# Block 1's mixers: POOL's tensor operations written for DVE, and the norm's factor applied in the copy out of PSUM

## The chip, the cores and the metric

The kernel runs on one core of a Trainium2 chip. The metric is device time in microseconds (us) of the whole program, lower is better. TensorE (PE, and PEld for its weight loads) multiplies matrices into PSUM; VectorE (DVE), ScalarE (ACT) and GpSimd (POOL) work element by element; SyncE (SP) issues the DMA transfers.

## The reference

Two transformer-like blocks on a sequence of 1024 tokens of width 1024, in float32. Only block 1's first half, the mixers, is touched by the change:

```python
h = rms_norm(x, norm_mix[l])
proj = jnp.einsum("bsd,dc->bsc", h, w_in[l])
q, k, v, z, b_f, b_b, a_f, a_b, su, sv = jnp.split(proj, SPLIT_POINTS, axis=-1)
qkv = jax.nn.silu(short_conv(jnp.concatenate([q, k, v], axis=-1), conv_w[l]))
o_a = bidir_gated_deltanet(qkv, z, b_f, b_b, a_f, a_b, ...)   # 8 heads of 64, chunks of 64
o_b = spatial_gating(su, sv, ...)                             # 4 groups of 128
x = x + jnp.einsum("bsc,cd->bsd", jnp.concatenate([o_a, o_b], axis=-1), w_out[l])
```

`rms_norm` multiplies each token by one factor, so the factor can be applied before the product with `w_in` or to the product. The delta rule solves a unit triangular system for each chunk, head and direction, and then runs over 16 chunks in order. After the mixers come block 1's feed-forward network and all of block 2 (an S5 state space layer, a gated convolution and a second feed-forward network).

## The kernel before

Tiles hold 128 channels by 1024 tokens, handled in two halves of 512 (`HS`). Every dense product is made of three float32r products: weight and input are both split into a high part (ACT copies it, line 318) and a low part (a subtraction, line 319), and hi·hi, hi·lo and lo·hi are summed in PSUM. `piece` loads one weight block (`wr`) and splits it (`wh`, `wl`); the engine of the subtraction is an argument. There are two buffers of `wr` and three each of `wh` and `wl`, so ACT's next `wh` waits until PE has used up an older one. Outputs of products go through two PSUM banks (`mm`), and for some of the products through two spare ones.

`norm0` splits the input and sums its squares over the 8 tiles (line 407) while the first products run; its factor per token is spread over the partitions in `rb`. The products are made on the unnormalised input, and the factor is multiplied in afterwards: `evac` copies both halves of a product out of PSUM on ACT (line 753) and POOL multiplies the copy by `rb` (line 754). `conv_tile` then makes one convolved tile of 128 channels: ACT the middle tap, DVE four taps (line 764), ACT a tanh, ACT adds 1 (line 767), POOL multiplies (line 768).

The heads go in four pairs. `pair_front` makes a pair's q, k and v, `pair_gdn` its delta rule: decays (DVE adds at line 901, POOL masks by `affine_select` at 905, ACT exponentials), Gram products, the inverse of the 32 by 32 diagonal blocks (31 steps of two DVE operations, lines 957 and 959, each step on the result of the last), the off-diagonal block, and the chain over the chunks (lines 1074 and 1077). Two pairs run at a time, pairs 0 and 1, then 2 and 3. `sgu_mix` makes the gated groups.

PE's program order is written out while the kernel is built: `drive` interleaves the steps of the two pairs, of the gated groups and of the dense products by constants for their latencies. The order on DVE, ACT and POOL is made by a scheduler from the same program; `late` and `at` bias it. Each engine works through its own order, and waits at an instruction whose inputs aren't there, with all that stands behind it.

Of the kernel before, what the change touches and what calls it, by code (L numbers as in the profile page):

```python
# [16 lines left out]
P = 128  # L17
# [234 lines left out]
class Kern:  # L252
# [69 lines left out]
    def front(self):  # L322
# [16 lines left out]
        with tc.manual_schedule(engines={mybir.EngineType.PE}):  # L339
            self.mark("norm")  # L340
            with self.pool("n0") as n0:
                self.norm0(n0)
            self.gp = es.enter_context(self.pool("gp", reuse_waits="tile"))
            self.gdn_consts()
            self.drive(self.dense(xes, res_es))
            self.tailw = [self.piece(I["w_out"], 2 * P, d * P, 2, G, 2 * P) for d in (0, 2, 4)]
        es.close()
        return self.res, res_es

    def norm0(self, n0):  # L350
# [16 lines left out]
        self.dma(self.ident, self.I["c_ident"])  # L367
        w0[2] = self.piece(wi, HF, 512, 4, G)
        w0[0] = self.piece(wi, 0, 2048, 8, G, 32, raw=n0.tile([P, HF], F32, name="wg"))
        load(0, (4, 6))  # L370
# [21 lines left out]
        for h in range(2):  # L392
# [3 lines left out]
            for d in range(KD):  # L396
# [9 lines left out]
                if d:  # L406
                    G.tensor_tensor(acc, acc, t, op=ALU.add)
                if h == 0:
# [58 lines left out]
    def mix_split(self, m, i, j):  # L467

        t = [self.rp.tile([P, S], F32R, tag=f"mx{i}{j}{e}", name="mix", bufs=1) for e in range(2)]
        for h in range(2):  # L470
            sl = self.HS[h]
            self.split(t[0][:, sl], t[1][:, sl], m[:, sl], (self.G, self.V)[(j + h) % 2])
        return t
# [105 lines left out]
    def wout(self, k0, mix, d, hs=(0, 1)):  # L579

        self.mark("wout")
        pss = yield from self.gprod(self.I["w_out"], k0 * P, d * P, mix, self.G, hs)
        for h, ps in zip(hs, pss):
# [47 lines left out]
    def proj(self, c0):  # L631
        if c0 in self.pre:
            return self.pre.pop(c0)
        return (yield from self.gprod(self.I["w_in"], 0, c0, self.x, self.G))

# [113 lines left out]
    def evac(self, pss, name):  # L749
        t = self.f4(name)  # L750
        with self.at(self.PR_EVAC):
            for h in range(2):
                self.A.activation(t[:, self.HS[h]], pss[h], AF.Copy)
        self.G.tensor_tensor(t, t, self.rb, op=ALU.mult)
        return t

    def conv_tile(self, j, raw, y):
# [8 lines left out]
        A.activation(raw, y, AF.Tanh)  # L766
        A.activation(raw, raw, AF.Copy, bias=1.0)
        self.G.tensor_tensor(y, raw, y, op=ALU.mult)
        return y
# [88 lines left out]
    def pair_gdn(self, p, st, R):  # L858
# [90 lines left out]
        for eg, dst in ((i_, i_), (K, Q)):  # L949
            self.late(A.activation(eg, eg, AF.Exp))  # L950
            G.tensor_tensor(dst, eg, Q, op=ALU.mult)
        for j in range(31, 0, -1):
# [15 lines left out]
        Y = [g, hs]  # L968
        for d, eng in ((0, V), (1, G)):
            eng.tensor_tensor(Y[d].rearrange("p (c e k) -> p c e k", e=2, k=32),  # L970
                              yc[:, d].unsqueeze(2).to_broadcast([P, NC, 2, 32]),
# [28 lines left out]
        for lo_, hi_ in zip(lo, hi):  # L1000
            A.activation(c3(Y[1])[hi_, :, 0:32], yp[hi_], AF.Copy, scale=-1.0)
        G.tensor_tensor(c3(K), c3(kp), bc(3), op=ALU.mult)

# [26 lines left out]
        for d in range(2):  # L1030
            G.tensor_tensor(c3(KW[d]), c3(kp), bc(4 + d), op=ALU.mult)
        one = lambda t, sl: t[:, sl].rearrange("p (c k) -> p c k", k=64)
# [140 lines left out]
    def sgu_mix(self):  # L1173
# [10 lines left out]
        for g in range(4):  # L1184
# [19 lines left out]
            v8 = vq.rearrange("p (n c) -> p n c", n=8)  # L1204
            G.tensor_tensor(v8, v8, r.unsqueeze(2).to_broadcast([P, 8, P]), op=ALU.mult)
            yield 0.0, self.LAT_SGU[1]
            t = vr
            for h in range(2):
                sl = self.HS[h]
                ps = yield from bank([P, 4, P], "mix")  # L1210
                for n in range(4):
# [4 lines left out]
                                       ws[:, 1:2, :].to_broadcast([P, 4, P]), op0=ALU.mult, op1=ALU.add)  # L1216
                G.tensor_tensor(gu[:, sl], gu[:, sl], t[:, sl], op=ALU.mult)
                A.activation(t[:, sl], gu[:, sl], AF.Square)
# [1108 lines left out]
```

## Time and profile before

| | us |
|---|---|
| median of 3 runs | 2793.81 (2791.37 to 2794.6) |
| the profiled execution | 2792.41 |
| its span, first to last instruction | 2790.5 |
| busy in the span: PE, DVE, ACT, POOL | 2616.2, 1861.0, 1076.9, 576.4 |

The mixers take about the first 795 us of the span. A stretch of the span is read by what is busy in it: an engine that is busy all the time sets the pace there, and a gap on PE is put down to the instruction that ended it.

### The profile page before, as it was taken

What the parts mean: (1) busy time and instruction counts of PE and PEld (TensorE: products, weight loads), DVE (VectorE), ACT (ScalarE), POOL (GpSimd) and SP (SyncE); (2) the same over time, 40 slices, a digit from 0 to 9 for tenths busy, and PEclk for the clock granted to TensorE, in tenths of its full rate; (3) what the DMA queues carried; (4) which work ended last, traced back from release to release, by engine and by line L of the source; (5) the groups of instructions that cost most, each with busy time, mean ns of one, the idle gap of its engine ahead of it and who ended that gap; (6) DMA issues with size and microseconds to landing.
All of it is one profiled execution on the core that took longest, in us unless ns stands there. A gap on an engine that the chain in (4) does not pass through costs nothing.

```text
span 2790.5 us, 39625 instructions
## 1 busy us (share of the span) xinstructions
PE 2616.2 (94%) x14952; PEld 2094.8 (75%) x14952; DVE 1861.0 (67%) x3174; ACT 1076.9 (39%) x1779; POOL 576.4 (21%) x671
## 2 busy tenths in 40 slices
PE   7777899889999999999999999989999999999997
PEld 4556677666777888888788888778876888888885
DVE  6889658865577666845547888666497555555446
ACT  4544443533264444422125443363245333352212
POOL 5764334523200000089910000100000000000010
PEclk8888999899999999999999999999999999999998
DMA  3332142213124333645422543554422222243211
GB/s 102 89 91 73 36 126 78 79 44 118 55 83 143 120 114 129 203 139 171 141 78 80 164 155 120 181 176 147 132 72 65 79 91 91 76 148 109 89 47 60
DMA packets 298623, 299.73 MB, mean 107 GB/s; under 512 B 34912, under 2 KB 243936, under 8 KB 298176
## 3 DMA queue, kind: packets, MB, share of 16 engines
q1 hardware_dynamic: 298432, 297.20, 34.2%
q8 instruction: 117, 1.92, 0.3%
q14 instruction: 74, 0.61, 0.1%
HBM read 222.29 MB, written 74.58 MB: 106 GB/s over the span
## 4 chain that ended last, share of the span: by engine, by line
PE 74%; DVE 17%; issue 3%; DMA 2%; ACT 2%; POOL 1%; SPq 1%; ACTq 0%; DVEq 0%; POOLq 0%
PE mm L1327 33%; PE mm L1300 28%; PE mm L611 5%; DVE h L959 2%; DVE stp L957 2%; PE wu L775 2%; DVE cy L764 1%; DVE fbgkq L764 1%; PE ob L775 1%; DVE xl L399 1%; PE mm L193 1%; DVE wl L319 1%; PE cp L775 1%; DVE res L216 1%; PE mm L1432 0%
## 5 line engine op out<-in xcount | busy, mean ns | idle before, releaser
L1327 PE MATMUL mm<-t,wh 128*128 128x512 f32 x1728 | 539.9, 393 | 11.3 <-DVE t L319 4.1
L318 ACT ACTIVATE wh<-wr 128x512 fp32r<-128x512 f32 (+1 forms) x386 | 236.0, 613 | 627.6 <-PE mm L1300 267.2
L1327 PEld LDWEIGHTS mm<-t,wh 128*128 128x128 f32 x1728 | 324.3, 188 | 88.5 <-DVE t L319 7.5
L1327 PE MATMUL mm<-b,wh 128*128 128x512 f32 x1232 | 382.5, 392 | 2.9 <-ACT acc L1368 2.9
L1300 PE MATMUL mm<-fh,wh 128*128 128x512 f32 x880 | 345.7, 393 | 4.8 <-DVE res L1508 4.8
L319 DVE TENSOR_TENSOR wl<-wr,wh 128x512 fp32r<-128x512 f32 (+1 forms) x311 | 219.4, 706 | 192.8 <-ACT wh L318 192.5
L1300 PE MATMUL mm<-fl,wh 128*128 128x512 f32 x880 | 343.2, 390 | 0.0
L1300 PE MATMUL mm<-fh,wl 128*128 128x512 f32 x880 | 343.0, 390 | 0.0
L1327 PE MATMUL mm<-t,wl 128*128 128x512 f32 x864 | 337.2, 390 | 0.0
L1327 PEld LDWEIGHTS mm<-b,wh 128*128 128x128 f32 x1232 | 231.5, 188 | 53.1 <-ACT acc L1368 4.0
L1327 PE MATMUL mm<-b,wl 128*128 128x512 f32 x616 | 240.2, 390 | 0.0
L318 ACT ACTIVATE wh<-ws 128x512 fp32r<-128x512 f32 x216 | 135.3, 630 | 252.8 <-PE mm L1327 232.0
L1300 PEld LDWEIGHTS mm<-fh,wh 128*128 128x128 f32 x880 | 165.5, 188 | 41.5 <-issue 5.2
L319 DVE TENSOR_TENSOR wl<-ws,wh 128x512 fp32r<-128x512 f32 x216 | 148.4, 690 | 71.2 <-ACT wh L318 70.8
L611 PE MATMUL mm<-xh,wh 128*128 128x512 f32 (+1 forms) x400 | 175.3, 438 | 21.7 <-ACT rows L826 7.1
L1300 PEld LDWEIGHTS mm<-fh,wl 128*128 128x128 f32 x880 | 165.6, 188 | 34.8
L1300 PEld LDWEIGHTS mm<-fl,wh 128*128 128x128 f32 x880 | 165.6, 188 | 34.4 <-issue 0.5
L1327 PEld LDWEIGHTS mm<-t,wl 128*128 128x128 f32 x864 | 162.8, 188 | 33.7
L319 POOL TENSOR_TENSOR wx<-wr,wx 128x512 fp32r<-128x512 f32 (+1 forms) x8 | 8.6, 1094 | 846.4 <-ACT wx L318 843.4
L611 PE MATMUL mm<-xl,wh 128*128 128x512 f32 (+1 forms) x400 | 172.8, 432 | 4.3 <-DVE xl L399 4.2
L611 PE MATMUL mm<-xh,wl 128*128 128x512 f32 (+1 forms) x400 | 171.7, 429 | 0.0
L319 POOL TENSOR_TENSOR wl<-wr,wh 128x512 fp32r<-128x512 f32 (+1 forms) x75 | 94.3, 1258 | 280.4 <-ACT wh L318 197.8
(498 smaller groups left out, 4758.1 us busy)
## 6 DMA issues: line engine op xcount, KB each, us to landing
wr<-in_w_ff SPq DMA_DIRECT2D x76, 256.0 KB
wr<-in_w_ff SPq DMA_DIRECT2D x32, 512.0 KB
fl<-ffd SPq DMA_DIRECT2D x32, 512.0 KB
wr<-in_w_in SPq DMA_DIRECT2D x32, 512.0 KB
wr<-in_w_in SPq DMA_DIRECT2D x60, 256.0 KB
wr<-in_w_gate SPq DMA_DIRECT2D x22, 512.0 KB
wr<-in_w_up SPq DMA_DIRECT2D x22, 512.0 KB
fl<-hd SPq DMA_DIRECT2D x22, 512.0 KB
```

The source lines that it names most:

```text
L193: K.T.matmul(st[:, e * n + k:e * n + k + 1], x[:, k * P:(k + 1) * P], K.ones[:, 0:1], start=e + i + k == 0, stop=i == 1, skip_group_check= ...
L216: K.V.tensor_tensor(r, r, self.mb, op=ALU.subtract)
L318: self.A.activation(hi, src, AF.Copy)
L319: return (lo_eng or self.V).tensor_tensor(lo, src, hi.bitcast(F32), op=ALU.subtract)
L399: V.scalar_tensor_tensor(xl[d][:, sl], xs[:, d, sl], g, xh[d][:, sl].bitcast(F32), op0=ALU.mult, op1=ALU.subtract)
L611: self.T.matmul(ps, a[:, t, :], b[:, sl], start=(first and j == 0), stop=(last and j == 2))
L764: V.scalar_tensor_tensor(y[:, a:b], raw[:, a + o:b + o], cw[:, k:k + 1], y[:, a:b], op0=ALU.mult, op1=ALU.add)
L775: self.T.matmul(out(s), lhsT(s), rhs(s), start=start, stop=stop)
L957: V.tensor_tensor(tm, X3[:, :, 0:j, j:j + 1].to_broadcast([P, 2, j, n]), T3[:, :, j:j + 1, m:16].to_broadcast([P, 2, j, n]), op=ALU.mult)
L959: V.tensor_tensor(T3[:, :, 0:j, m:16], T3[:, :, 0:j, m:16], tm, op=ALU.subtract)
L1300: self.T.matmul(ps, a, b[:, sl], start=(start and k + j == 0), stop=(stop and k == n - 1 and j == 2))
L1327: self.T.matmul(ps, a[:, k, :], b, start=(start and k + j == 0), stop=(k == 3 and j == 2), skip_group_check=True)
```

## The change

In the mixers every POOL operation on two tensors is written for DVE: the low parts of the weights and of the mixers' outputs, the sums of squares, and the products of the delta rule and of the gated groups. `evac` reads PSUM on DVE and multiplies by `rb` on the way, so that ACT's copy and POOL's multiplication become one DVE instruction for each half. The end of `conv_tile`, (tanh + 1) times y, becomes one DVE instruction in place of one of ACT and one of POOL. POOL keeps `affine_select`, memory fills, one weight block at the mixers' end and its work in block 2.

```diff
@@ norm0 @@
-        w0[2] = self.piece(wi, HF, 512, 4, G)
-        w0[0] = self.piece(wi, 0, 2048, 8, G, 32, raw=n0.tile([P, HF], F32, name="wg"))
+        w0[2] = self.piece(wi, HF, 512, 4, V)
+        w0[0] = self.piece(wi, 0, 2048, 8, V, 32, raw=n0.tile([P, HF], F32, name="wg"))
...
-                    G.tensor_tensor(acc, acc, t, op=ALU.add)
+                    V.tensor_tensor(acc, acc, t, op=ALU.add)
@@ mix_split @@
-            self.split(t[0][:, sl], t[1][:, sl], m[:, sl], (self.G, self.V)[(j + h) % 2])
+            self.split(t[0][:, sl], t[1][:, sl], m[:, sl], self.V)
@@ wout, and the same in proj @@
-        pss = yield from self.gprod(self.I["w_out"], k0 * P, d * P, mix, self.G, hs)
+        pss = yield from self.gprod(self.I["w_out"], k0 * P, d * P, mix, self.V, hs)
@@ evac @@
-                self.A.activation(t[:, self.HS[h]], pss[h], AF.Copy)
-        self.G.tensor_tensor(t, t, self.rb, op=ALU.mult)
+                self.V.tensor_tensor(t[:, self.HS[h]], pss[h], self.rb[:, self.HS[h]], op=ALU.mult)
@@ conv_tile @@
-        A.activation(raw, raw, AF.Copy, bias=1.0)
-        self.G.tensor_tensor(y, raw, y, op=ALU.mult)
+        V.scalar_tensor_tensor(y, raw, 1.0, y, op0=ALU.add, op1=ALU.mult)
@@ pair_gdn, and the same at 1002 and 1031 @@
-            G.tensor_tensor(dst, eg, Q, op=ALU.mult)
+            V.tensor_tensor(dst, eg, Q, op=ALU.mult)
...
-        for d, eng in ((0, V), (1, G)):
-            eng.tensor_tensor(Y[d].rearrange("p (c e k) -> p c e k", e=2, k=32),
+        for d in range(2):
+            V.tensor_tensor(Y[d].rearrange("p (c e k) -> p c e k", e=2, k=32),
@@ sgu_mix, and the same at 1217 @@
-            G.tensor_tensor(v8, v8, r.unsqueeze(2).to_broadcast([P, 8, P]), op=ALU.mult)
+            V.tensor_tensor(v8, v8, r.unsqueeze(2).to_broadcast([P, 8, P]), op=ALU.mult)
```

The order of instructions on PE is the same in both programs. On DVE, where pair 0's inverse begins (`stp` and `h` are its steps, `cy` a convolved tile of another pair, `wl` the low part of a weight block, `raw<-mm` a product read from PSUM), there stood before:

```order
L832 SCALAR_TENSOR_TENSOR rows<-rows,vecs,grow 32x1024
L957 TENSOR_TENSOR stp<-fbgkq,h 128x62
L959 TENSOR_TENSOR h<-h,stp 128x2x31
L957 TENSOR_TENSOR stp<-fbgkq,h 128x60
L959 TENSOR_TENSOR h<-h,stp 128x2x30
L957 TENSOR_TENSOR stp<-fbgkq,h 128x116
L959 TENSOR_TENSOR h<-h,stp 128x2x29x2
L957 TENSOR_TENSOR stp<-fbgkq,h 128x112
L959 TENSOR_TENSOR h<-h,stp 128x2x28x2
L957 TENSOR_TENSOR stp<-fbgkq,h 128x162
L959 TENSOR_TENSOR h<-h,stp 128x2x27x3
```

and there stands now:

```order
L830 SCALAR_TENSOR_TENSOR rows<-rows,vecs,grow 32x1024
L319 TENSOR_TENSOR wl<-wr,wh 128x512
L955 TENSOR_TENSOR stp<-fbgkq,h 128x62
L753 TENSOR_TENSOR raw<-mm,rb 128x512
L766 SCALAR_TENSOR_TENSOR cy<-raw,cy 128x1024
L753 TENSOR_TENSOR raw<-mm,rb 128x512
L957 TENSOR_TENSOR h<-h,stp 128x2x31
L319 TENSOR_TENSOR wl<-wr,wh 128x512
L848 COPY col<-cps 64x8x6 x4
L955 TENSOR_TENSOR stp<-fbgkq,h 128x60
L763 SCALAR_TENSOR_TENSOR cy<-raw,cwh,cy 128x1022
L957 TENSOR_TENSOR h<-h,stp 128x2x30
```

Between two steps of the inverse there are now reads of products, low parts and a convolution's last step, each of them an instruction that waits for ACT or PE. On POOL, from pair 0's masks to pair 1's, there stood before:

```order
L905 AFFINE_SELECT ca<-ca 64x1024 x2
L905 AFFINE_SELECT fbgkq<-fbgkq 64x1024 x2
L905 AFFINE_SELECT ca<-ca 64x1024 x2
L905 AFFINE_SELECT de<-de 64x1024 x2
L319 TENSOR_TENSOR wl<-wr,wh 128x512 x2
L754 TENSOR_TENSOR raw<-raw,rb 128x1024
L768 TENSOR_TENSOR fbgkq<-raw,fbgkq 128x1024
L319 TENSOR_TENSOR wl<-wr,wh 128x512
L951 TENSOR_TENSOR i<-i,fbgkq 128x1024
L319 TENSOR_TENSOR wl<-wr,wh 128x512
L754 TENSOR_TENSOR raw<-raw,rb 128x1024
L951 TENSOR_TENSOR fbgkq<-fbgkq 128x1024
```

and there stands now, from the same masks on:

```order
L903 AFFINE_SELECT ca<-ca 64x1024 x2
L903 AFFINE_SELECT fbgkq<-fbgkq 64x1024 x2
L903 AFFINE_SELECT ca<-ca 64x1024 x2
L903 AFFINE_SELECT de<-de 64x1024 x2
L903 AFFINE_SELECT ca<-ca 64x1024 x2
```

Pair 1's masks now follow pair 0's with nothing between them; the low parts, the products with `rb` and the convolutions' last steps stand in DVE's order.

## Rows read from the trace of the kernel before

**Rows 1.** The page: busy tenths of DVE and POOL in 40 equal slices of the span.

```profile
DVE  6889658865577666845547888666497555555446
...
POOL 5764334523200000089910000100000000000010
```

**Rows 2.** Busy time by stretch of the mixers: PE, PEld, DVE, ACT, POOL (count), clock, DMA.

```profile
159.10:310.50 151.40, 110.53 (x838) 85.30 (x836) 148.47 (x199) 62.56 (x89) 82.04 (x41) 0.84 0.25 72
...
428.00:474.90 46.90, 43.90 (x492) 31.17 (x487) 44.74 (x133) 14.27 (x21) 11.74 (x6) 0.93 0.10 25
...
528.30:584.20 55.90, 38.01 (x282) 29.05 (x281) 52.45 (x97) 20.56 (x37) 24.40 (x13) 0.82 0.08 24
584.20:795.00 210.80, 195.44 (x2122) 144.83 (x2122) 119.37 (x296) 72.25 (x142) 56.72 (x48) 0.94 0.24 81
sum 795.00, PE 667.97 PEld 497.18 DVE 582.35 ACT 328.53 POOL 350.91; mean PE 95.42 PEld 71.03 DVE 83.19 ACT 46.93 POOL 50.13
```

**Rows 3.** The chain that ended last, 159 to 310 us, by line.

```profile
by line: DVE h L959 25.5%; DVE stp L957 22.4%; DVE cy L764 17.8%; issue 4.4%; DVE fbgkq L946 3.0%; DVE fbgkq L947 2.8%; DVE fbgkq L970 2.6%; DVE rows L832 2.3%; DVE ca L901 2.2%; DVE rows L828 1.8%; DVE ca L927 1.6%; DVE fbgkq L967 1.5%; DV
```

**Rows 4.** Timeline, single instructions: start, duration, engine, line, operation [idle before].

```profile
6.65 0.69 DVE L319 TENSOR_TENSOR wl<-wr,wh 128x512 fp32r<-128x512 f32 x1 [0.52 <-ACT wh L318]
...
213.20 1.27 DVE L764 SCALAR_TENSOR_TENSOR cy<-raw,cwh,cy 128x1023 f32<-128x1023 f32 x1
...
460.68 0.36 DVE L957 TENSOR_TENSOR stp<-fbgkq,h 128x192 f32<-128x192 f32 x1
...
468.22 0.16 DVE L312 SCALAR_TENSOR_TENSOR qt<-qt,qa 128x8 f32<-128x8 f32 x1
...
471.89 1.87 DVE L312 SCALAR_TENSOR_TENSOR qt<-qt,qa 128x8 f32<-128x8 f32 x1
...
471.00 2.73 POOL L970 TENSOR_TENSOR h<-fbgkq,half 128x1024 f32<-128x1024 f32 x1 [7.63 <-DVE fbgkq L965]
...
565.26 1.22 DVE L1228 TENSOR_TENSOR sv<-ident,qy 128x1024 f32<-128x1024 f32 x1
```

**Rows 5.** Groups of DVE, 159.1 to 310.5 us: busy, mean ns, idle before.

```profile
L959 DVE TENSOR_TENSOR h<-h,stp 128x252 f32<-128x252 f32 (+22 forms) x62 | 43.2, 706 | 1.0
L957 DVE TENSOR_TENSOR stp<-fbgkq,h 128x252 f32<-128x252 f32 (+22 forms) x62 | 37.2, 608 | 1.1
L764 DVE SCALAR_TENSOR_TENSOR cy<-raw,cwh,cy 128x1023 f32<-128x1023 f32 (+1 forms) x18 | 29.3, 1627 | 0.1
```

**Rows 6.** Groups of POOL, 159.1 to 310.5 us.

```profile
L319 POOL TENSOR_TENSOR wl<-wr,wh 128x512 fp32r<-128x512 f32 x13 | 21.1, 1622 | 52.6 <-ACT wh L318 45.0 <-DMA fbgkq<-rd 7.5
L754 POOL TENSOR_TENSOR raw<-raw,rb 128x1024 f32<-128x1024 f32 x5 | 13.9, 2781 | 0.1
L768 POOL TENSOR_TENSOR cy<-raw,cy 128x1024 f32<-128x1024 f32 x5 | 12.3, 2470 | 9.9 <-ACT raw L767 6.3 <-DVE stp L957 2.6 <-POOL wl L319 0.8
L905 POOL TENSOR_SCALAR_AFFINE_SELECT ca<-ca 64x1024 f32<-64x1024 f32 x4 | 6.6, 1657 | 1.6 <-DVE ca L901 1.5
...
L754 POOL TENSOR_TENSOR z<-z,rb 128x1024 f32<-128x1024 f32 x2 | 5.7, 2869 | 0.5 <-ACT z L753 0.5
```

**Rows 7.** Groups of DVE and ACT, 0 to 795 us.

```profile
L585 DVE TENSOR_TENSOR res<-mm,res 128x512 f32<-128x512 f32 x40 | 27.6, 689 | 30.0 <-PE mm L611 29.6
...
L753 ACT ACTIVATE raw<-mm 128x512 f32<-128x512 f32 x24 | 14.0, 586 | 7.0 <-DVE z L1142 4.5 <-PE mm L611 2.5
L767 ACT ACTIVATE raw<-raw 128x1024 f32<-128x1024 f32 x12 | 12.6, 1051 | 0.2
```

**Rows 8.** Waits, 0 to 795 us: us in total, times, longest.

```profile
POOL wl L319 <- ACT wh L318: 197.8, 41, 15.3
...
ACT sv L753 <- PE mm L611: 12.4, 2, 6.4
...
PE l L819 <- ACT raw L807: 11.2, 3, 6.7
...
PE rb L390 <- DVE dg L384: 7.7, 1, 7.7
```

More of the change, by code (lines that the diff above doesn't have):

```diff
@@ L345, in front @@
             self.drive(self.dense(xes, res_es))
-            self.tailw = [self.piece(I["w_out"], 2 * P, d * P, 2, G, 2 * P) for d in (0, 2, 4)]
+            self.tailw = [self.piece(I["w_out"], 2 * P, d * P, 2, V, 2 * P) for d in (0, 2, 4)]
         es.close()
@@ L633, in proj @@
             return self.pre.pop(c0)
-        return (yield from self.gprod(self.I["w_in"], 0, c0, self.x, self.G))
+        return (yield from self.gprod(self.I["w_in"], 0, c0, self.x, self.V))
     def slots_of(self, R, i):
@@ L1001, in pair_gdn @@
             A.activation(c3(Y[1])[hi_, :, 0:32], yp[hi_], AF.Copy, scale=-1.0)
-        G.tensor_tensor(c3(K), c3(kp), bc(3), op=ALU.mult)
+        V.tensor_tensor(c3(K), c3(kp), bc(3), op=ALU.mult)
         self.mark(f"wu{p}")
@@ L1030, in pair_gdn @@
         for d in range(2):
-            G.tensor_tensor(c3(KW[d]), c3(kp), bc(4 + d), op=ALU.mult)
+            V.tensor_tensor(c3(KW[d]), c3(kp), bc(4 + d), op=ALU.mult)
         one = lambda t, sl: t[:, sl].rearrange("p (c k) -> p c k", k=64)
@@ L1216, in sgu_mix @@
                                        ws[:, 1:2, :].to_broadcast([P, 4, P]), op0=ALU.mult, op1=ALU.add)
-                G.tensor_tensor(gu[:, sl], gu[:, sl], t[:, sl], op=ALU.mult)
+                V.tensor_tensor(gu[:, sl], gu[:, sl], t[:, sl], op=ALU.mult)
                 A.activation(t[:, sl], gu[:, sl], AF.Square)
```

## The prediction

> **What bounds the kernel now.** Only the mixers change, some 795 of 2790.5 us. I read the page first: POOL's busy slices are those of the mixers, and a few of the S5 stage far behind [rows 1]. DVE is at 8 or 9 tenths in some slices of the mixers and at half in others, so I cut the mixers into stretches at the ends of the pairs' inverses. PE is busy 668 of 795 us in all. In three stretches DVE is what is full: 148.5 of 151.4 us (pairs 0 and 1 in their inverses), 44.7 of 46.9 and 52.5 of 55.9 (pairs 2 and 3) [rows 2]. In the first, PE is idle for 41 us, and the granted clock is 0.84, which is 1.2 instead of 2.4 GHz for about a third of it. The chain of waits agrees: steps of the inverse and convolutions alone are 66% of it [rows 3]. Behind the last inverse it is the other way round: PE is busy 195 of 211 us [rows 2].
>
> Then the single instructions show why DVE is full. A Newton step on 8 columns takes 0.16 us; the same step takes 1.87 us where a POOL multiplication of 2.73 us has just begun [rows 4]. Steps of the inverse take 0.61 and 0.71 us in the mean [rows 5]; a lone one of 192 columns (their mean is 184) takes 0.36 [rows 4]. Convolution taps take 1.63 in the mean against 1.27 [rows 4, 5]. Operations that read PSUM don't show it: 40 additions to `res` in a mean of 0.69, the time of a lone 512-column subtraction [rows 4, 7]. So DVE's full time is partly waiting for POOL, and POOL is slow in return: 1.62 us for a low part that DVE makes in 0.69.
>
> **The change part by part.** I work it out for the stretch from 159 to 310 us, since DVE's load there decides.
>
> What DVE gets back: 62 steps on each line at 0.36 are 22.3 us, against 43.2 and 37.2, so 20.9 and 14.9; 18 taps at 1.27 are 22.9 against 29.3, so 6.4 [rows 4, 5]. The other groups with two inputs in SBUF are too small for a row each; I put them at 6, bounds 2 (hardly touched) and 10. About 48 us.
>
> What DVE takes on: of POOL's 41 instructions, 8 are masks, which stay. 13 low parts at 0.69 are 9.0. Seven tiles out of PSUM, two halves each at 0.69 (nearest row: the additions to `res`, one input in PSUM, one in SBUF), are 9.7. Five last steps of the convolution at 1.27 (nearest row: a tap, the same kind of instruction) are 6.4. The other 8, full-width multiplications, at 1.22 are 9.8 [rows 2, 4, 6, 7]. Together 35 us.
>
> What stays: 8 masks, 1.66 us each in the mean, can each hold up one DVE operation [rows 6]. Between 0 and 13 us; I take 5, since DVE's decay additions and PSUM reads stand around them, and only some are hit.
>
> So DVE's load there falls by 48 - 35 - 5 = 8 us, with bounds of a fall of 20 and a rise of 5. That DVE loses work that it never had, and gets nearly as much of real work, is the heart of this case: freed and added almost cancel.
>
> The other two full stretches have POOL busy 36 us against 82 [rows 2]. Scaled by that, the same sum gives 4; both have inverses with little convolution, where a long POOL operation stops a short step, so I take 6, bounds 0 and 15.
>
> Norm: PE waits 7.7 us for DVE's `dg` [rows 8]. Fourteen additions at 0.69, 9.7 us, come into DVE's order, and the splits beside them lose their waiting. Bounds 0 and 7.7, taken as 4.
>
> Fronts: PE waits 11.2 us in three goes for the squares of a convolved tile [rows 8]. On the way to one stood 0.59 (copy, ACT), 2.78 (POOL), 1.05 (ACT) and 2.47 (POOL); now 0.69 and 1.27 [rows 4, 6, 7]: 4.9 us shorter for each tile. It would cover all three waits if DVE were free at once; half the time it isn't. I take 5, bounds 0 and 11.
>
> The rest of the mixers: PE is busy nearly throughout; shorter hops in the gated groups and outputs are mostly hidden behind its products; I take 3, bounds 0 and 8. ACT loses 48 copies (12 tiles of q, k and v, and 4 each of z, su and sv, two halves each) at 0.59 and 12 additions at 1.05, some 41 us; it is nowhere full (62.6 of 151.4 us [rows 2]), so I count nothing for it.
>
> The loads of weights on SP's queue are the same in number and move by a place or two; DMA is busy a quarter of the worked stretch [rows 2], so nothing is counted for them.
>
> New waits: 75 low parts (counted in POOL's order before) and the 48 reads of products now stand in DVE's order. A read waits for PE's product, a low part for ACT's `wh` and so for PE to give up a buffer. POOL waited 197.8 us at its low parts, 41 times, and nobody minded; ACT waited 12.4 us at two reads of `sv` [rows 8]. On DVE the inverse's next step and the chain's next state stand behind such a wait, and PE's Gram, level and chain products behind those. Where DVE lags, as in the full stretches, the wait is already over when DVE gets there; where it leads, it has time. A third of these 123 instructions lie in the full stretches (254 of 795 us), some 40. At a quarter of a microsecond each that is 10 us, which I take; bounds 0 and 45 (every fourth held for POOL's mean wait of 4.8).
>
> Sum: -8 - 6 - 4 - 5 - 3 + 10 = -16, on the profiled execution's 2792.4: 2776. The median of the runs shown lies 1.4 above it, so **2778**.
>
> The Trainium skill speaks against a part of this: "Perfetto Trace Analysis", section "Optimizing Scalar/DVE Operations", has it that with DVE saturated, work may better go to ScalarE or GpSimd, and here copies leave ScalarE for a DVE that is full. In the worked stretch the rows make that a price: seven tiles cost DVE 9.7 us that ACT had room for. Were they kept on ACT, with the multiplication by `rb` on DVE at 1.22 a tile (8.5 us), DVE would save only 1.2 us; so the rule is right in sign, and by it the sum would be 1.2 better without this part.
>
> **The rivals.** *A wash.* The freed 48 and the added 35 are from the same trace but one is waiting and one is work; if the masks cost 13 instead of 5 and the holds 25 instead of 10, the sum is -16 + 8 + 15 = +7 less what DVE's empty time absorbs, so about 0: 2790 to 2798. For it: DVE's load hardly changes. Against it: the tiles' way is shorter by 4.9 us in any case. The same section of "Perfetto Trace Analysis" says that moving operations between GPSIMD and DVE might not help, as they share a port; by that rule alone the time would stay at 2794.
>
> *Slower: DVE held at the head of its queue.* Place: the full stretches, at reads and low parts ahead of a step of the inverse. The gains are 26 us; with 40 such instructions it decides at 0.65 us each. At 45 us in all the time is 2792.4 + 19 = 2811, some 2813 in the median. For it: PE runs at 1.2 GHz for a third of that stretch, so what DVE waits for comes late, and ACT's waits for PE show that a queue does get held at such reads. Against it: low parts are made about one product ahead, since there are three buffers.
>
> *Much faster.* If DVE runs through without holds, and PE's 41 us of gaps in the first full stretch shrink enough that the clock stays at 2.4 GHz, half of the 48 us at 1.2 GHz would come back as up to 12 us more there, and as much elsewhere: 2792.4 - 26 - 24 = 2742, some 2744. Against it: PE has to wait for DVE in these stretches whatever its clock.
>
> **How the numbers follow.** The runs of before spread by 3.2 us; within 0.2%, or 5.6 us, I call it the same. Chances: the forecast, 6 to 30 us faster, 0.50; faster than that, 0.12; a wash, 0.16; slower by more, 0.22. So faster 0.62, same 0.16, slower 0.22. The range leaves out about one in ten at each end: from the upper part of the much faster case, 2750, to half of the slower case, 2803.
>
> **What the changed kernel's profile would show.** Right: no DVE step of the inverse above 0.5 us except beside a mask; their mean near 0.36; DVE still nearly full from 159 to about 300 us; reads by `rb` near 0.69; the end of pair 1's inverse 10 to 25 us earlier than 310; PE's waits for squares and for `dg` smaller. Wrong, if DVE's idle time ahead of the reads and low parts is above 30 us in the full stretches, if PE waits for `wl` or for a bank of `mm` that DVE hasn't read, or if steps of the inverse still take 0.6 us without POOL beside them, which would mean that the waiting had another cause.

## The result, and the profile after

The changed kernel takes 2756.12 us in the median of four runs (2753.74 to 2759.49), beside 2792.59 for the kernel before (2786.45 to 2794.6, four runs): a ratio of 0.9874, 95% interval 0.9854 to 0.9893. It is 36 us faster, where 16 was forecast. Run once more beside later experiments it came to 0.9868 (0.9853 to 0.9883). The profiled execution took 2753.74 us, its span 2751.8, each 38.7 less than before. Of all the executions in this document one, of the last experiment (7227 us, where the others of that kernel took 2748 to 2762), is left out of its comparison.

The page first, the slices that answer to [rows 1].

```profile
DVE  7899768865696566655548778666597555564456
...
POOL 0220011000000000299700001100000000000010
```

POOL is empty in the mixers but for the masks. DVE's slices look much as they did: up to the last edge that I use, just behind the mixers, the engine is busy 614.4 of 798.2 us, where it was 621.8 of 838.2. These two rows stand last in the next two answers. The view is busy time by stretch, in columns PE, PEld, DVE, ACT, POOL (count), granted clock, DMA share, GB/s. The stretches end at the same instructions in both kernels: DVE's `dg` in the norm (the diagonal matrix by which PE spreads the norm's factor over the partitions), the last `rows` step of pair 0's front, and the starts and ends of the pairs' inverses. The last edge, 838.2 and 798.2, is where PE takes up the `dg` of the next norm, the feed-forward network's; the mixers' last product ends some 25 us ahead of it, at 813.4 before and at 773.4 now, so the 795 us that I called the mixers stop a little short of their end. First the kernel before, for the stretches that [rows 2] doesn't have:

```profile
0.00:39.80 39.80, 21.21 (x65) 11.72 (x65) 33.00 (x38) 19.76 (x33) 25.64 (x23) 0.80 0.46 142
39.80:109.50 69.70, 59.37 (x235) 42.85 (x236) 46.86 (x42) 35.42 (x45) 36.30 (x20) 0.89 0.21 56
...
0.00:838.20 838.20, 709.96 (x6452) 532.38 (x6452) 621.79 (x1113) 355.45 (x573) 350.91 (x214) 0.90 0.28 82
```

and the changed kernel, where 142.40, 399.70 and 496.10 answer to 159.10, 428.00 and 528.30 in [rows 2]:

```profile
0.00:32.50 32.50, 17.72 (x65) 10.22 (x65) 26.23 (x54) 19.55 (x33) 2.34 (x9) 0.99 0.55 174
32.50:94.40 61.90, 58.70 (x236) 43.11 (x237) 46.72 (x63) 28.04 (x33) 1.05 (x3) 0.92 0.23 63
...
142.40:283.80 141.40, 107.93 (x863) 83.77 (x863) 133.21 (x238) 52.01 (x75) 13.86 (x8) 0.86 0.26 77
...
399.70:441.70 42.00, 37.50 (x425) 26.76 (x421) 39.53 (x128) 10.39 (x13) 0.00 (x0) 0.96 0.08 21
...
496.10:547.30 51.20, 40.67 (x320) 31.82 (x321) 45.10 (x112) 21.61 (x39) 0.00 (x0) 0.90 0.09 27
...
0.00:798.20 798.20, 695.30 (x6452) 525.21 (x6452) 614.37 (x1306) 322.64 (x515) 55.73 (x45) 0.93 0.28 86
```

From these edges the 38.7 us can be split. In the three full stretches the time of DVE is split once more, into busy (245.7 us before, 217.8 now) and idle (8.5 before, 16.8 now).

| part | forecast, us | measured, us | from |
|---|---|---|---|
| norm, to `dg` | -4 | -7.3 | 39.8 to 32.5 |
| fronts, `dg` to the first inverse | -5 | -9.4 | 119.3 to 109.9 |
| full stretches, load of DVE | -8 and -6 | -15.3 and -12.6 | busy 148.5 to 133.2; 97.2 to 84.6 |
| full stretches, holds | +10 | +8.2 | idle 8.5 to 16.8 |
| the other stretches, to the last edge | -3 | -3.7 | 424.9 to 421.2 |
| behind that edge | 0 | +1.3 | the rest of the span |
| sum | -16 | -38.7 | |

In the first full stretch the groups of DVE stand so (they answer to [rows 5], and for the work taken over to [rows 6]; line numbers are 1 or 2 lower than before):

```profile
L763 DVE SCALAR_TENSOR_TENSOR cy<-raw,cwh,cy 128x1023 f32<-128x1023 f32 (+1 forms) x18 | 23.0, 1278 | 0.2 <-ACT cy L759 0.2
L955 DVE TENSOR_TENSOR stp<-fbgkq,h 128x252 f32<-128x252 f32 (+22 forms) x62 | 21.8, 365 | 0.8
L957 DVE TENSOR_TENSOR h<-h,stp 128x252 f32<-128x252 f32 (+22 forms) x62 | 21.8, 362 | 0.8
L319 DVE TENSOR_TENSOR wl<-wr,wh 128x512 fp32r<-128x512 f32 x13 | 9.9, 758 | 0.5 <-ACT wh L318 0.4
L766 DVE SCALAR_TENSOR_TENSOR cy<-raw,cy 128x1024 f32<-128x1024 f32 x5 | 7.0, 1407 | 0.0
L753 DVE TENSOR_TENSOR raw<-mm,rb 128x512 f32<-128x512 f32 x8 | 5.5, 689 | 5.3 <-DMA vtd<-cy 4.5 <-PE mm L611 0.7
...
L753 DVE TENSOR_TENSOR z<-mm,rb 128x512 f32<-128x512 f32 x4 | 2.7, 687 | 0.0
```

The steps of the inverse, 0.71 and 0.61 us before, take 0.36; the 62 on each line 43.6 us in place of 80.4. Taps take 1.28 in place of 1.63. Low parts, reads and the convolutions' ends have lengths near the forecast's 0.69, 0.69 and 1.27. The chain of waits, by line, in the first full stretch, beside [rows 3]:

```profile
by line: DVE stp L955 12.0%; DVE h L957 11.6%; DVE cy L763 11.3%; issue 10.2%; DMA vtd<-cy 6.2%; DVE wl L319 4.4%; SPq L873 4.1%; DVE cy L766 3.1%; PE wu L773 2.9%; DVE ca L925 1.9%; DVE ca L899 1.9%; DMA kqd<-cy 1.8%; DVE z L753 1.8%; DVE 
```

Steps and taps were 66% of the chain and are now 35%; the read that waits for a DMA store, low parts and convolution ends have come in, but none of them is large.

### The profile page after: what moved, and what is told of

It is laid out like the page before. It is cut to its first block, busy times and chain, and to the rows that moved or that the text cites. A ratio compares the mean times of both kernels' runs of the same rounds, so it can differ in the third digit from the quotient of the medians.

```text
span 2751.8 us, 39513 instructions
## 1 busy us (share of the span) xinstructions
PE 2602.0 (95%) x14952; PEld 2088.2 (76%) x14952; DVE 1854.9 (67%) x3367; ACT 1044.6 (38%) x1721; POOL 279.5 (10%) x502
## 4 chain that ended last, share of the span: by engine, by line
PE 75%; DVE 14%; DMA 3%; ACT 3%; issue 3%; POOL 1%; SPq 1%; ACTq 0%; DVEq 0%; POOLq 0%
PE mm L1325 34%; PE mm L1298 26%; PE mm L611 6%; PE wu L773 2%; DVE wl L319 1%; DVE stp L955 1%; DVE h L957 1%; DVE cy L763 1%; PE ob L773 1%; PE cp L773 1%; DVE res L216 1%; PE mm L1430 0%; DVE res L215 0%; PE mm L193 0%; DVE t L319 0%
## 5 line engine op out<-in xcount | busy, mean ns | idle before, releaser
L319 DVE TENSOR_TENSOR wl<-wr,wh 128x512 fp32r<-128x512 f32 (+1 forms) x385 | 267.4, 695 | 214.1 <-ACT wh L318 212.9
L319 DVE TENSOR_TENSOR wl<-ws,wh 128x512 fp32r<-128x512 f32 x216 | 148.5, 690 | 70.2 <-ACT wh L318 69.9
L1506 DVE TENSOR_TENSOR res<-mm,res 128x512 f32<-128x512 f32 x128 | 85.8, 683 | 74.1 <-PE mm L1298 74.1
L1325 PEld LDWEIGHTS mm<-b,wl 128*128 128x128 f32 x616 | 115.9, 188 | 24.5
```

The lines of the kernel that those rows point to most:

```text
L319: return (lo_eng or self.V).tensor_tensor(lo, src, hi.bitcast(F32), op=ALU.subtract)
L1325: self.T.matmul(ps, a[:, k, :], b, start=(start and k + j == 0), stop=(k == 3 and j == 2), skip_group_check=True)
L1506: V.tensor_tensor(res[d][:, sl], self.mm(w, ffs[g], sl), res[d][:, sl], op=ALU.add)
```

## The experiments

Three reasons could stand behind the gain. **Waiting given back**: DVE's two-tensor steps waited for POOL's two-tensor operations, and every such operation that leaves POOL frees DVE. **A shorter way**: a product goes from PSUM to its convolution in fewer hops, whatever POOL does. **Holds**: what low parts and reads cost at the head of DVE's queue.

### The three parts of the change, each alone

From the kernel before, first only the low parts (`piece`, `gprod` and `mix_split` with V in place of G, lines 346, 368, 369, 472, 582 and 634):

```diff
-        pss = yield from self.gprod(self.I["w_out"], k0 * P, d * P, mix, self.G, hs)
+        pss = yield from self.gprod(self.I["w_out"], k0 * P, d * P, mix, self.V, hs)
```

> The kernel before with one part of the change alone: the low parts of weights and of the mixers' outputs are made on DVE, nothing else moves. Theory 1 (DVE's steps were waiting for POOL's two-tensor operations, and each that goes gives time back): the low parts were 21 of POOL's 82 us in the stretch from 159 to 310 us, so a quarter to a third of the gain, 6 to 14 us faster than before; steps of the inverse come down from 0.61 and 0.71 us, but not to 0.36, since POOL's multiplications by rb and the convolutions' ends are still there. Theory 2 (the gain is the shorter way of a product through its copy and the end of its convolution): nothing of that way is touched, 0 us, within 4 either way. Theory 3 (low parts in DVE's order hold it up at ACT's wh, the forecast's 10 us, of which some two thirds are low parts): 0 to 8 us slower, with DVE idle ahead of its low parts for more than 10 us in the full stretches.

Second only the reads and the end of the convolution:

```diff
-                self.A.activation(t[:, self.HS[h]], pss[h], AF.Copy)
-        self.G.tensor_tensor(t, t, self.rb, op=ALU.mult)
+                self.V.tensor_tensor(t[:, self.HS[h]], pss[h], self.rb[:, self.HS[h]], op=ALU.mult)
...
-        A.activation(raw, raw, AF.Copy, bias=1.0)
-        self.G.tensor_tensor(y, raw, y, op=ALU.mult)
+        V.scalar_tensor_tensor(y, raw, 1.0, y, op0=ALU.add, op1=ALU.mult)
```

> The kernel before with one part of the change alone: products are read from PSUM on DVE with the factor on the way, and the convolution's end, (tanh + 1) times y, is one DVE instruction; the low parts and the rest stay on POOL. Theory 1 (waiting given back): POOL loses some 32 of its 82 us from 159 to 310 us and DVE takes on 16; with the shorter way of the convolved tiles in the fronts, 10 to 22 us faster than before; the steps of the inverse still 0.4 to 0.55 us, beside POOL's low parts. Theory 2 (shorter way): nearly the whole gain, 25 to 36 us faster. Theory 3 (holds): reads hold DVE for 3 us at most here, nothing to tell.

Third only the rest, seven lines from G to V (407, 951, 969, 1002, 1031, 1205, 1217):

```diff
-                    G.tensor_tensor(acc, acc, t, op=ALU.add)
+                    V.tensor_tensor(acc, acc, t, op=ALU.add)
...
-            G.tensor_tensor(dst, eg, Q, op=ALU.mult)
+            V.tensor_tensor(dst, eg, Q, op=ALU.mult)
```

> The kernel before with what is left of the change alone: the sums of squares in the norm, the delta rule's products and the gated groups' products are made on DVE; low parts, the products' multiplication by rb and the convolutions' ends stay on POOL. Theory 1 (waiting given back): the norm's 5 to 7 us, and 2 to 6 us in the full stretches, 6 to 13 us faster. Theory 2 (shorter way of a product): none of it is here, 0 us, within 4 either way. If the three parts alone come to much less than the 36.5 us of the whole change (below 22), the parts need one another: as long as some of POOL's two-tensor operations are left, DVE waits at them.

| kernel | median, us | ratio to before | interval | gain, us |
|---|---|---|---|---|
| low parts alone | 2776.63 | 0.9950 | 0.9937 to 0.9963 | 14 |
| reads and ends alone | 2769.16 | 0.9921 | 0.9909 to 0.9933 | 22 |
| the rest alone | 2770.92 | 0.9929 | 0.9917 to 0.9941 | 20 |

(The kernel before stood at 2791.46 on this chip, nine runs; a gain is one minus the ratio, times that.) Each part gains alone, so the shorter way of a product isn't the whole reason: two of the three don't touch it. (DVE also makes each operation in less time than POOL did, a low part in 0.69 us against 1.62, and what needs its result can start sooner by that. These three runs don't part that from the waiting given back; the runs with useless work on POOL, below, show the waiting by itself.) The low parts gain although DVE is idle 15.5 us at them waiting for `wh` in this kernel, as the first row below shows. In all three the steps of the inverse, on lines that had 609 and 535 ns over the whole mixers before, come down to 470 to 500 without reaching the 356 and 358 of the changed kernel. Groups of DVE in the first 755 us, in which all 124 steps of each line lie; before:

```profile
L959 DVE TENSOR_TENSOR h<-h,stp 128x252 f32<-128x252 f32 (+22 forms) x124 | 75.0, 609 | 2.1
L957 DVE TENSOR_TENSOR stp<-fbgkq,h 128x252 f32<-128x252 f32 (+22 forms) x124 | 65.8, 535 | 2.3
```

the changed kernel:

```profile
L957 DVE TENSOR_TENSOR h<-h,stp 128x252 f32<-128x252 f32 (+22 forms) x124 | 43.5, 356 | 1.9
L955 DVE TENSOR_TENSOR stp<-fbgkq,h 128x252 f32<-128x252 f32 (+22 forms) x124 | 43.5, 358 | 1.9
```

low parts alone:

```profile
L319 DVE TENSOR_TENSOR wl<-wr,wh 128x512 fp32r<-128x512 f32 (+1 forms) x75 | 64.6, 861 | 21.2 <-ACT wh L318 15.5 <-PE mm L611 4.3 <-issue 0.8
L957 DVE TENSOR_TENSOR stp<-fbgkq,h 128x252 f32<-128x252 f32 (+22 forms) x124 | 58.1, 475 | 2.0
L959 DVE TENSOR_TENSOR h<-h,stp 128x252 f32<-128x252 f32 (+22 forms) x124 | 57.9, 473 | 1.9
```

reads and ends alone:

```profile
L955 DVE TENSOR_TENSOR stp<-fbgkq,h 128x252 f32<-128x252 f32 (+22 forms) x124 | 59.3, 480 | 2.4
L957 DVE TENSOR_TENSOR h<-h,stp 128x252 f32<-128x252 f32 (+22 forms) x124 | 58.1, 470 | 2.3
```

the rest alone:

```profile
L959 DVE TENSOR_TENSOR h<-h,stp 128x252 f32<-128x252 f32 (+22 forms) x124 | 61.2, 499 | 2.1
L957 DVE TENSOR_TENSOR stp<-fbgkq,h 128x252 f32<-128x252 f32 (+22 forms) x124 | 61.0, 497 | 2.0
```

The third part's 20 us are more than any theory gave it. At the norm's `dg` it is 6.4 us ahead of before already, where the whole change is 7.2 ahead (see the sums of squares below). And the three gains together are 56 us, against 35 to 37 for the whole: I had written down what it would mean if they came to much less, and they came to more. The steps show the same: the parts free 24.8, 23.4 and 18.6 us of them, 66.8 in all, and the whole frees 53.8 (140.8 to 87.0). What one part frees, another would have freed too.

### The low parts as the last part

The changed kernel with only the low parts put back on POOL (the six lines of the first part; one is shown), which says what the part is worth when the others are already there. The changed kernel itself ran beside it.

```diff
-        pss = yield from self.gprod(self.I["w_out"], k0 * P, d * P, mix, self.V, hs)
+        pss = yield from self.gprod(self.I["w_out"], k0 * P, d * P, mix, self.G, hs)
```

> The changed kernel with one part undone: the low parts are made on POOL again, all else stays as changed. The three parts alone gave 15, 22 and 20 us, which is 57 for a whole of 36.5. If they overlap because the time that DVE waits for POOL shrinks faster than POOL's work (parts one by one count the same waiting twice), this kernel has nearly all of the gain, 30 to 36 us faster than before, with the steps of the inverse at 0.40 to 0.46 us. If the parts add up and only the last one, the low parts, costs again what it gives (DVE held at wh, the forecast's 10 us, and 75 low parts more of DVE's own work), this kernel is faster than the changed one, 37 us or more faster than before. If low parts on POOL make DVE wait as the extra subtractions on POOL did (17 us for 46 of them), it is 10 to 20 us slower than the changed kernel.

> The changed kernel once more, beside the others on the same chip: 0.986 to 0.989 of the kernel before. It is the mark against which the 5 to 9 us of the masks, the store and the low parts are read.

It took 2759.74 us, 0.9893 (0.9878 to 0.9908); the changed kernel 2753.78, 0.9868 (0.9853 to 0.9883). The low parts are worth 6 or 7 us as the last part and 14 as the first. The intervals overlap a little, and the gain of this kernel, 30 us, stands at the edge of the first expectation; that the parts overlap is what fits, and the other two expectations miss. The steps take 0.39 and 0.40 us, just below what was expected. Here DVE is busy less than in the changed kernel (598.7 us up to the last edge, at 805.9; 614.4 up to 798.2), and the last edge still comes 7.7 us later:

```profile
0.00:805.90 805.90, 697.49 (x6452) 525.49 (x6452) 598.66 (x1223) 323.00 (x515) 161.97 (x128) 0.93 0.28 85
```

So it isn't DVE's load, summed over the mixers, that sets the time.

### Copy out of PSUM on ACT

```diff
-                self.V.tensor_tensor(t[:, self.HS[h]], pss[h], self.rb[:, self.HS[h]], op=ALU.mult)
+                self.A.activation(t[:, self.HS[h]], pss[h], AF.Copy)
+        self.V.tensor_tensor(t, t, self.rb, op=ALU.mult)
```

> The changed kernel with the products' copy out of PSUM back on ACT (two halves) and the multiplication by rb as one full-width DVE instruction in SBUF. By the rows of before a tile then costs DVE 1.22 instead of 1.38 us. Theory 1 (what counts is that POOL has no two-tensor operation): most of the gain stays; DVE's load falls by 0.16 us a tile, the way of a tile is 0.6 us and one hop longer: 0 to 8 us slower than the changed kernel, 28 to 36 faster than before. Theory 2 (the gain is the shorter way): a good part of it goes, 12 us or more slower than the changed kernel. The Trainium skill (Perfetto Trace Analysis, Optimizing Scalar/DVE Operations) has that with DVE saturated work may better go to ScalarE: by that rule it would be 1 to 3 us faster than the changed kernel.

2756.13 us, 0.9868 (0.9853 to 0.9883): the changed kernel's time. Reading PSUM with the factor on the way, the most visible piece of the diff, is worth nothing that these runs can tell (the interval is some 4 us to either side) against a copy on ACT and a multiplication on DVE. That speaks against the shorter way once more, at least this hop of it. The 1 to 3 us that I had worked out by the rule of the Trainium skill ("Perfetto Trace Analysis", section "Optimizing Scalar/DVE Operations") are too small for this comparison.

### Work put back on POOL that nobody needs

Two kernels, both from the changed one. After a weight block of four pieces is split, POOL either subtracts `wh` from it again (one operation on two tensors), or fills it twice with a constant. The results aren't used. (The lines that set `spoil` for the mixers are left out.)

```diff
+        if getattr(self, "spoil", None) and cols == P and m == 4:
+            self.G.tensor_tensor(raw, raw, hi.bitcast(F32), op=ALU.subtract)
```

```diff
+        if getattr(self, "spoil", None) and cols == P and m == 4:
+            for _ in range(2):
+                self.G.memset(raw, 0.0)
```

> The changed kernel, in which POOL does extra work that nobody uses: for each weight block of four pieces in the mixers it subtracts the high part from the raw block again, in place, a two-tensor operation in SBUF, after ACT and DVE have read the block. The block's buffer comes free later by that. No output changes. Theory 1 (a two-tensor operation on POOL makes DVE's two-tensor steps wait): the steps of the inverse go from 0.36 back above 0.45 us in the mean in the full stretches, and the kernel is 8 to 25 us slower than the changed one. Theory 2 (shorter way): nobody waits for POOL's result, so no more than 3 us slower, and the steps stay at 0.36.

> As the run before, but POOL fills the same block twice with a constant instead of subtracting: the same hold of the block's buffer, POOL is busy, but reads no tensor. No output changes. Theory 1 in its narrow form (what DVE waits for is POOL reading tensors): steps of the inverse stay at 0.36 us, within 3 us of the changed kernel. Theory 1 in a wide form (any busy POOL slows DVE): slower by as much as in the run before. A hold of the block's buffer as the cause: both runs are slower alike, with waits of DMA for POOL and none of the steps longer.

The subtractions: 2766.6 us, 0.9916 (0.9902 to 0.9930), 12 to 13 us slower than the changed kernel. The fills: 2749.09, 0.9856 (0.9841 to 0.9870), not slower, if anything 3 to 5 us faster, which the intervals don't tell from nothing. The changed kernel didn't run beside these two, and is compared by its ratios, 0.9868 and 0.9874. Side by side the two differ by 17 us. On POOL, the subtractions in the mixers:

```profile
L604 POOL TENSOR_TENSOR wr<-wr,wh 128x512 f32<-128x512 f32 x46 | 72.1, 1568 | 414.1 <-DVE wl L319 250.7 <-issue 105.8 <-DVE h L961 16.7
```

and the fills:

```profile
L605 POOL MEMSET wr<- 128x512 f32 x92 | 48.4, 527 | 422.2 <-DVE wl L319 369.3 <-issue 32.5 <-ACT raw L810 17.8
```

On DVE, with the subtractions beside:

```profile
L959 DVE TENSOR_TENSOR stp<-fbgkq,h 128x252 f32<-128x252 f32 (+22 forms) x124 | 52.0, 422 | 2.0
...
L961 DVE TENSOR_TENSOR h<-h,stp 128x252 f32<-128x252 f32 (+22 forms) x124 | 46.6, 380 | 1.8
```

and with the fills beside:

```profile
L960 DVE TENSOR_TENSOR stp<-fbgkq,h 128x252 f32<-128x252 f32 (+22 forms) x124 | 45.2, 368 | 2.1
L962 DVE TENSOR_TENSOR h<-h,stp 128x252 f32<-128x252 f32 (+22 forms) x124 | 44.0, 360 | 1.8
```

46 operations of POOL whose results nobody waits for lengthen the steps to 422 and 380 ns and cost 12 us and more; 48 us of fills leave them at 368 and 360. Both kernels hold the weight block's buffer, for 1.57 us at a time or for two fills of 0.53, and the hold isn't the cause: ACT's waits for the weights' transfers, ahead of `wh` in the first 800 us, are 14.9 us with the subtractions, 24.6 with the fills and 23.2 in the changed kernel, and all its idle time there is 155.3, 165.1 and 158.6. The steps stayed below the 0.45 us that I had expected; only 46 operations were put back, not all that POOL had before. This is the run that shows the waiting as a cause, and not only as something that went away with the work. The Trainium skill, "SBUF — State Buffer", section "Who interferes with whom", has that a DVE instruction with two inputs in SBUF contends with a GpSimd instruction that reads SBUF, and not with one that only writes it. The two runs agree: 17 us between them.

### The sums of squares back on POOL

```diff
-                    V.tensor_tensor(acc, acc, t, op=ALU.add)
+                    G.tensor_tensor(acc, acc, t, op=ALU.add)
```

> The changed kernel with one piece undone: the norm's sums of squares are added on POOL again. Theory 1: the norm's end comes later by most of the 7 us that it came earlier, 3 to 7 us slower than the changed kernel, with the splits beside the additions longer. Rival: the norm's gain came from the low parts of the first weights, which left POOL too, and the additions may be anywhere: within 2 us of the changed kernel.

2767.41 us, 0.9920 (0.9902 to 0.9938), 13 to 15 us slower than the changed kernel, compared by the ratios as before, and twice what I expected; the norm's `dg` comes 8.3 us later, so the 14 additions alone hold the whole gain of the norm, and some 5 us go elsewhere. The groups of DVE up to `dg`, in this kernel:

```profile
L399 DVE SCALAR_TENSOR_TENSOR xl<-xs,vecs,xh 128x512 fp32r<-128x512 f32 x16 | 22.5, 1447 | 3.7 <-ACT xh L398 3.7
```

and in the changed kernel:

```profile
L399 DVE SCALAR_TENSOR_TENSOR xl<-xs,vecs,xh 128x512 fp32r<-128x512 f32 x16 | 11.6, 750 | 2.7 <-ACT xh L398 2.7
L407 DVE TENSOR_TENSOR acc<-acc,t 128x512 f32<-128x512 f32 x14 | 9.6, 688 | 0.0
```

With the additions on POOL a split of the input takes DVE 1.45 us; with the additions among its own work 0.75. DVE does 9.6 us more and is through sooner.

### The masks on DVE, and a store on another queue

What POOL still does in the mixers is masks. They stand in each other's way with DVE, as the timeline of the changed kernel shows where pair 1's masks begin (start, duration, instruction); on DVE:

```profile
183.64 1.22 DVE L899 TENSOR_TENSOR fbgkq<-fbgkq,col 128x1024 f32<-128x1024 f32 x1
...
186.85 2.15 DVE L899 TENSOR_TENSOR de<-de,col 128x1024 f32<-128x1024 f32 x1
188.93 1.33 DVE L955 TENSOR_TENSOR stp<-fbgkq,h 128x240 f32<-128x240 f32 x1
```

and on POOL:

```profile
183.84 4.09 POOL L903 TENSOR_SCALAR_AFFINE_SELECT ca<-ca 64x1024 f32<-64x1024 f32 x2 [62.92 <-DVE ca L899]
```

The same addition takes 1.22 us or 2.15, and a lone step of the inverse 1.33. The candidate: a minimum with a small triangle, made once (the lines that make it are left out below), in place of each pair of half masks.

```diff
-                for hh in range(2):
...
-                    G.affine_select(c3(rb)[sl], c3(rb)[sl], pattern=[[0, NC], [sg, 64]], compare_op=ALU.is_ge,
-                                    fill=NEG, base=0, channel_multiplier=-sg)
+                V.tensor_tensor(c3(rb), c3(rb), self.tri[:, d, :].unsqueeze(1).to_broadcast([P, NC, 64]), op=ALU.min)
```

> The changed kernel with the decays' masks made on DVE too, by a minimum with a small prepared triangle; POOL makes no mask in the mixers. 16 masks of half the partitions become 8 DVE instructions of 1.22 us, some 10 us more on DVE, 4.9 of them in the first full stretch. Theory 1: DVE's operations beside the masks, 1.2 to 2.15 us each in the changed kernel, go back to their own length, and the chain loses POOL's masks, so 2 to 6 us faster than the changed kernel. Rival: masks on POOL lay beside DVE's own work and DVE is full there, so the new work costs 3 to 6 us.

> The changed kernel with the masks as a minimum on DVE, once more, beside the changed kernel on the same chip. If the 8 us that it gained are its own, it is 5 to 10 us faster than the changed kernel here too; if they came from the chip or the order of the DMA transfers, within 3.

2747.12 us, 0.9844 (0.9830 to 0.9859), and again 2749.11, 0.9844 (0.9829 to 0.9858), where the changed kernel beside it had 0.9868: by the ratios 7 to 8 us faster than the changed kernel, by the medians of the two that ran side by side 4.7, just short of the 5 to 10 expected there. The intervals overlap by 0.0005, so the size isn't settled. It is the fastest version here by the ratios, 43 us faster than the kernel before, and the gain is near or above the upper end of the 2 to 6 us that I expected at first. I had counted half of the masks: 32 half masks became 16 DVE instructions, 19.6 us, and it still gains. Most of it, 4.7 us, is there when pair 0's inverse begins (137.7 us in place of 142.4), behind pair 0's masks. In the first full stretch an addition and a mask now take 1.22 us each:

```profile
L906 DVE TENSOR_TENSOR ca<-ca,col 128x1024 f32<-128x1024 f32 x2 | 2.4, 1218 | 0.0
L907 DVE TENSOR_TENSOR ca<-ca,tri 128x1024 f32<-128x1024 f32 x2 | 2.4, 1216 | 0.0
```

The last run added one line to it, which moves the stores of convolved tiles from SP's DMA queue to ACT's:

```diff
-                    self.dma(st["dst"][i], y)
+                    self.nc.scalar.dma_start(st["dst"][i], y)
```

> The changed kernel with the masks on DVE, and the stores of finished convolved tiles issued on ACT's DMA queue in place of SP's. In the changed kernel DVE is held 4.5 us, once, at the head of its queue in the first full stretch, at a read whose buffer a store still needs, and that store stood behind eight broadcast loads on SP's queue. If the hold is the queue's, DVE's wait there goes and the kernel is 2 to 5 us faster than with the masks alone; if the transfers themselves are full (DMA is busy at 8 or 9 tenths there), the same within 2 us.

2755.99 us, 0.9866 (0.9846 to 0.9886), by the medians 7 us slower than with the masks alone, though the intervals overlap. The hold for the store went, as one theory had it, and another came, at ACT's `wh`. Of the waits of DVE up to the end of the first full stretch, with the masks alone:

```profile
DVE raw L760 <- DMA vtd<-cy: 4.5, 1, 4.5
...
DVE wl L319 <- ACT wh L318: 1.2, 2, 0.7
```

and with the store on ACT's queue:

```profile
DVE wl L319 <- ACT wh L318: 5.0, 3, 3.8
```

So neither expectation came out. That ACT's `wh` is later because ACT now issues the stores is my reading; it wasn't tried apart.

## Why the prediction was right in direction and too small

**The mechanism** was right: DVE's full time was partly waiting for POOL. The steps came to 0.36 us, the taps to 1.28, the reads to 0.69, each as written, and the two runs with useless work on POOL show the cause. Of all the steps of the inverse that stand alone in the first full stretch only two took above 0.5 us, 1.33 and 1.18, both while POOL made pair 1's masks. The inverse of pair 1 ends 26.7 us earlier, a little beyond the 10 to 25 that I gave. **The sizes** failed: the time lies in the range, above its lower end by 6 us, and is 22 us below the forecast. By the table every term of the mixers came out better than forecast, within its own bounds and four of them near the favourable end, where I had taken the middle. The largest miss is the load of DVE in the full stretches: -14 forecast, -27.8 measured.

**Load in the first full stretch, -8 forecast, -15.3 measured.** What I took as freed is nearly right: steps 36.8 us (35.8 forecast), taps 6.3 (6.4), the other groups some 4 (6). What I took as added is too: 13 low parts 9.9 (9.0), 12 reads 8.2 (9.7 for 14), five ends 7.0 (6.4), the full-width multiplications 9.5 (9.8). The term that was mis-sized is the 5 us for masks. Decay additions that a mask holds up were as long before, so they are no loss:

```profile
L970 DVE TENSOR_TENSOR fbgkq<-fbgkq,half 128x1024 f32<-128x1024 f32 x2 | 4.1, 2050 | 0.0
...
L901 DVE TENSOR_TENSOR de<-de,col 128x1024 f32<-128x1024 f32 x1 | 2.2, 2157 | 0.0
```

and in the changed kernel:

```profile
L968 DVE TENSOR_TENSOR fbgkq<-fbgkq,half 128x1024 f32<-128x1024 f32 x2 | 2.4, 1217 | 0.0
...
L949 DVE TENSOR_TENSOR i<-i,fbgkq 128x1024 f32<-128x1024 f32 x1 | 2.2, 2153 | 0.0
L899 DVE TENSOR_TENSOR de<-de,col 128x1024 f32<-128x1024 f32 x1 | 2.2, 2152 | 0.0
```

Newly held are one product (2.15 in place of 1.22), low parts (0.76 in place of 0.69) and ends (1.41 in place of 1.22), together some 3, and the measured lengths above hold them already. Full-width operations such as the first row of each answer (2.05 to 1.22) were in the 6 us put down for what was too small for a row. Added up from the timeline, DVE's durations in the stretch fall by 11.4 us, 156.3 to 145.0, where the sum had 8 (and by its own bounds 17 at most, not 20). The other 3.9 us lie in the measure: busy time counts only once what two instructions overlap, 7.9 us before, with 199 instructions, and 11.8 now, with 238, where the forecast added up durations.

**Load in the other two, -6 forecast, -12.6 measured.** Here a step of the working failed: I scaled the first stretch's sum by POOL's busy time, 36 us to 82, which puts what is freed at 21 us and what is added, masks with it, at 17.6. By the durations in the timeline DVE took on 17.6 us indeed, but some 28 were freed (108.7 to 97.5 in all; busy time falls a little more, as above). Half of all steps lie in these two stretches, and fell by 17.0 us there (53.8 over the mixers); the Newton steps on 8 columns (lines 311 and 312) fell by some 5.5 and the chain's steps (line 1074) by 3.0. Counting such operations stretch by stretch would have come nearer than POOL's share.

**Holds, +10 forecast, +8.2 measured**, the best of the terms. In the full stretches DVE is idle 9.3 us ahead of reads and low parts: 5.6 in the first, the rest at reads of `sv`; at 30 I would have called the prediction wrong. The waits in the first stand in its rows above: 4.5 us for a DMA store, 0.7 for a product, 0.4 for `wh`.

Elsewhere they are longer (DVE waits 19.9 us at low parts in the first 755), outside the three stretches in which DVE is full. So the holds neither vanished nor turned the sign; the rival in which they decide needed 0.65 us for each of 40, some 26 us.

**Norm, -4 forecast, -7.3 measured.** The number lies inside my bounds; what failed is the reason for them. I let the gain end at PE's wait of 7.7 us for `dg` [rows 8], and that wait is still 5.5 us. What became shorter lies ahead of it: 16 splits of 1.48 us became 0.75 while 14 additions were added, and the whole of the norm came earlier.

**Fronts, -5 forecast, -9.4 measured.** I priced one wait, PE's for the squares, and took half of it. Most of it is gone from this stretch, and so is half of another that I had not priced, the one for `rows`, further along the same way. PE is busy as long as before there (100.9 us, was 101.4); its idle time fell from 17.9 to 9.0. Waits of PE from the norm to the first inverse, before:

```profile
PE l L819 <- ACT raw L807: 9.3, 2, 6.7
...
PE mm L611 <- ACT rows L826: 7.1, 1, 7.1
```

and in the changed kernel:

```profile
PE rb L390 <- DVE dg L384: 5.5, 1, 5.5
PE mm L611 <- ACT rows L824: 3.6, 1, 3.6
PE l L817 <- issue: 3.0, 1, 3.0
```

9.3 us became 3.0 (without a releaser that the profile shows), and 7.1 became 3.6: together 9.8 us, all of the 9.4. So half of the squares' wait was near (6.3 us; another of 5.5 now stands in the first full stretch, where 1.9 stood), and the term that the sum lacked is the 3.5 us at `rows`.

**The rivals.** A wash is out: moving work from POOL to DVE gained 36 us. "Perfetto Trace Analysis" in the Trainium skill, section "Optimizing Scalar/DVE Operations", has it that moving operations between those two might not help, since they share a port; this case's measurement goes the other way, since what POOL and DVE held up in each other went away with the move. The slower case is answered by the holds above. The much faster case came nearer in size (2744), but for a reason that the first full stretch doesn't bear out: the granted clock there is 0.86, and was 0.84. Up to the last edge it is 0.93 in place of 0.90, and PE is busy 14.7 us less for the same 6452 matmuls. But in the second profile of the changed kernel, whose last edge comes 2.1 us later, PE is busy 6.4 us more than in the first, so the two numbers don't go together well enough to say how much of the gain is the clock's. That stays open.

## What to carry to other kernels

Where DVE is full and POOL is busy beside it, first look at one short DVE instruction alone and beside a POOL operation: where it was twice as long and more, as here, what POOL did "for nothing" was paid by DVE, and giving DVE the work cost little. Count such steps in each stretch, not a stretch's share of POOL's time, and don't end a gain at the wait of one instruction when all that lies ahead of it becomes shorter. Gains of the parts of such a change overlap (14, 22 and 20 us here for a whole of 36), so a part must be judged with the others in place.

## What was unexpected of the hardware

A POOL operation whose result nobody uses slowed the kernel: 46 subtractions of 1.57 us cost 12 us and more, while 92 fills cost nothing that can be told. `affine_select`, which reads its tensor and writes it, made an addition of DVE beside it take 2.15 us in place of 1.22. And the same program can have PE busy 695.3 or 701.7 us up to the last edge used here with only 2.1 us between the times of that edge.
